# A hybrid decoder step: keys kept in token order, and the last weighting of a head pair put three slots after its weights

## Chip, cores and metric

One core of a Trainium2 chip runs the whole step. The metric is the device time of one execution in microseconds, the median of the runs shown; lower is better. One execution was also profiled, and its rows stand further down.

## What is computed

One layer for a prompt of 2048 tokens and a group of 8 samples with 4 new tokens each, model width 1024. The layer adds three mixers to its input through one output projection, and then a feed-forward network with a short convolution:

```python
x <- x + W_out[ concat(A, B, C) ](RMSNorm(x));   x <- x + ConvFFN(RMSNorm(x))
# A: 8 heads x 64, three (window, dilation) patterns, keys at distances 0, d, 2d, ..
PATTERNS = ((128, 1), (512, 4), (2048, 16))
oa = combine_dilations([dilated_band_prompt(qa, ka, va, slopes, w, d) for w, d in PATTERNS])
# combine_dilations:
mx = max over the patterns; num = sum(n * exp(m - mx)); den = sum(d * exp(m - mx)); out = num / den
# B: gated DeltaNet, 4 heads, chunks of 64;   C: cross-attention, 4 heads, 256 memory tokens
```

The keys of mixer A, after their RMS norm, are also an output (`win_k_prompt`), and so is every value row.

## The kernel before

**Precision.** A dense product is made of three matmuls (`mm3`, lines 294 to 296): a high part and a low part of each operand, the high part written by the Scalar engine (ACT), the low part by a subtraction on the Vector engine (DVE) or, for some weights, on GpSimd (POOL) (`weight`, lines 285 and 287).

**First stage** (`dense_in`, up to about 1040 us): the input projection of four blocks of 512 tokens, the DeltaNet, and the attention of the first 512 queries (`pair`, chunk 0). `head_norm` scales the heads' keys and queries; its `finish` makes the last product (line 499) and stores it. For keys the product is written into another tile (`vt`), its 512 tokens turned from token order into residue order (16 residues of 32 tokens), and stored so in `kT`. `vt` is a tag of three buffers; the values' evacuations (line 589), which come next in `ORDER`, need it too.

**Second stage** (`feed`): output projection and feed-forward network of one block after the other, and beside it the attention of the next block's 512 queries (chunks 1 to 3, three in all), issued in slots: `tick` lets one slot be issued after a share of the dense chunks. In `attn` a chunk's four head pairs and two cross pairs are a list of stages; stage k starts in slot k, and each of its functions stands one slot after the one before it. A head pair has six stages: load, far, middle (two halves), near (two halves). Its load splits the keys of two blocks for each of two heads (`ksplit`, lines 1130 and 1131, after `dup` has loaded `nat`, a tag of two buffers), four splits a pair. `far_scores` (line 1495) multiplies single residues of queries and keys, 256 matmuls a chunk as the trace counts them.

**The end of a pair.** `combine` (from line 1512) works out the weights of the two partial sums from small tiles, turns them on TensorE, copies them on ACT (`wt`, line 1535), sends them to DRAM (`wd`, line 1537) and brings them back spread over 128 partitions (`W`, line 1540). `finish_pair` then multiplies both partial sums by `W` on DVE (`os` line 1549, `nf` line 1550), adds them on POOL (line 1551) and stores the sum. `nf` has one buffer; the next pair's `mid_out` writes it from PSUM (`evac`, line 1088 on DVE). `add_halves` (line 1324, POOL) adds the two halves of `E` after their exponentials; TensorE transposes that sum (line 1319).

**Order.** The code's order gives priorities alone: a scheduler that runs when the kernel is built sets every engine's order, from its own estimates of the operations. Each engine and the queue of SyncE (SP), which issues all DMAs, then runs in that order, and what waits holds up what stands behind it.

Of the kernel before, what the change touches and what calls it, by code (L numbers as in the profile page):

```python
# [10 lines left out]
F32 = mybir.dt.float32  # L11
# [9 lines left out]
SEQ = 2048  # L21
# [44 lines left out]
def constants():  # L66
# [30 lines left out]
    with np.errstate(divide='ignore'):  # L97
# [8 lines left out]
        key = np.concatenate([128 * t + tok for t in range(4)])  # L106
        c['lbias'] = np.stack([bias(p[:, None] + 384 - key[None, :], sl) for sl in slopes])
        near = p[:, None] + 128 - key[None, 0:256]
# [97 lines left out]
def finish(r):  # L206
    y = r['yT'].reshape(D, TOT).T
    kT = r['kT'].reshape(512, TOT)
    kp = kT[:, :SEQ].reshape(512, SEQ // 512, 16, 32).transpose(0, 1, 3, 2).reshape(512, SEQ)
    kk = np.ascontiguousarray(np.concatenate([kp, kT[:, SEQ:]], 1).T)  # L210
# [19 lines left out]
class Body:  # L230
# [225 lines left out]
    def head_norm(self, srcs, xs, r4, w, gain, dsts, pre=(), turned=False):  # L456
# [31 lines left out]
        def finish():  # L488
            for x, raw in enumerate(raws):
                out = self.vt()[:, 0:w] if turned else raw  # L490
                for lo in range(0, w, 512):
# [3 lines left out]
                    o, i = out[:, lo:hi], raw[:, lo:hi]  # L495
                    if turned and lo == 0:
                        o = o.rearrange('p (r i) -> p i r', r=16)
                        i, ps = (t.rearrange('p (i r) -> p i r', r=16) for t in (i, ps))
                    nc.vector.scalar_tensor_tensor(out=o, in0=i, scalar=gain, in1=ps, op0=ALU.mult, op1=ALU.mult)
                for d, sl in dsts[x]:  # L500
                    nc.sync.dma_start(d, out[:, sl])
# [63 lines left out]
    def dense_in(self, b, xsr):  # L565
# [36 lines left out]
        def heads(c0, n, gain, dst, r4, pre=()):  # L602
            cols = lambda d: [(d[:, t0:t1], slice(0, npt))] + ([(d[:, SEQ:TOT], slice(npt, w))] if samp else [])
            return self.head_norm([A['w_ct'][c0 + x] for x in range(n)], xs, r4, w, gain, [cols(dst[x]) for x in range(n)], pre, dst is A['kT'])
# [475 lines left out]
    def neg(self, out, in_):  # L1080
        self.nc.vector.tensor_scalar(out=out, in0=in_, scalar1=-1.0, scalar2=None, op0=ALU.mult)
# [46 lines left out]
    def ksplit(self, src, kh, kl):  # L1128
        t = self.dup(src)
        self.nc.scalar.activation(kh, t, AF.Identity)  # L1130
        self.nc.vector.tensor_tensor(out=kl, in0=t, in1=kh.bitcast(F32), op=ALU.subtract)
# [70 lines left out]
    def cross_wide(self, c, hp):  # L1202
# [14 lines left out]
        def scores(n0):  # L1217
# [9 lines left out]
            self.neg(st[:, 0], st[:, 0])  # L1227
# [29 lines left out]
    def pair_load(self, c, hp):  # L1257
# [3 lines left out]
        for par in range(2):  # L1261
# [3 lines left out]
            for j in range(nb):  # L1265
                sl = slice(j * 512, j * 512 + 512)
                self.ksplit(self.A['kT'][hp, pr, (j0 + j) * 512:(j0 + j) * 512 + 512], *(t[:, sl] for t in K[par]))
        K = [[t.rearrange('p (b r i) -> p b r i', b=nb, r=16) for t in k] for k in K]
# [4 lines left out]
    def pair(self, c, hp):  # L1273
# [3 lines left out]
        v = self.values_of(range(4), cols)  # L1277
# [655 lines left out]
```

## Time and profile before

| | us |
|---|---|
| median of 3 runs | 2933.63 (2927.24 to 2937.6) |
| the profiled execution | 2932.09 |
| its span in the profile | 2930.3 |
| TensorE busy (matmul) | 2810.9, 96% |
| DVE, ACT, POOL busy | 2124.8, 1299.4, 902.2 |
| mean granted TensorE clock | 0.98 |

The span is the time from the first to the last instruction of the profiled execution; 1.8 us lie around it. The share of an engine is a mean over stages that differ, so the rows further down take it by stage. A granted clock of 1.00 is 2.4 GHz; parts of a stretch at 0.5 (1.2 GHz) pull its mean down.

### The profile page before, as it was taken

The numbers are of one execution on the slowest core, as the hardware profiler recorded it, in microseconds if no ns is written. First come the engines' busy times: TensorE is split into PE (matmuls) and PEld (weight loads), VectorE is DVE, ScalarE is ACT, GpSimd is POOL, SyncE is SP. The second block draws the span as 40 slices with busy tenths as digits, with TensorE's granted clock in tenths as the row PEclk, the third lists the DMA queues.
The fourth block names the chain that finished last, engine by engine and source line by source line (L and its number), as shares of the span: only waits on it lengthen the run. The fifth ranks groups of instructions, "written<-read, shape, count | busy, mean of one in ns | idle before, by whom it ended". The sixth has DMA issues, their size and how long they took to land. (4 is left out here: it accounts for less than half of the span.)

```text
span 2930.3 us, 55986 instructions
## 1 busy us (share of the span) xinstructions
PE 2810.9 (96%) x20702; PEld 2351.8 (80%) x20702; DVE 2124.8 (73%) x4696; ACT 1299.4 (44%) x2813; POOL 902.2 (31%) x1142
## 2 busy tenths in 40 slices
PE   8998989999989998999999989999899999999999
PEld 7778878777767777777677877777778778999999
DVE  7876747868756878778366888866877776666666
ACT  6545426546534435544233555435444433433332
POOL 3421302311312424333123343322333322333332
PEclk9999989999989999999999999999999999999999
DMA  5545423533434345544855545455444335232223
GB/s 175 161 133 95 141 82 125 165 111 115 130 109 131 97 117 147 152 139 132 269 180 169 151 142 150 137 170 171 135 151 140 103 93 168 94 90 91 87 87 102
DMA packets 275778, 390.88 MB, mean 133 GB/s; under 512 B 83952, under 2 KB 153744, under 8 KB 275504
## 3 DMA queue, kind: packets, MB, share of 16 engines
q1 hardware_dynamic: 275504, 387.29, 44.0%
q8 instruction: 164, 2.69, 0.4%
q14 instruction: 110, 0.90, 0.1%
HBM read 341.87 MB, written 45.32 MB: 132 GB/s over the span
## 5 line engine op out<-in xcount | busy, mean ns | idle before, releaser
L285 ACT ACTIVATE wh<-raw 128x512 fp32r<-128x512 f32 (+2 forms) x778 | 483.5, 626 | 716.4 <-PE facc L295 562.3
L294 PE MATMUL facc<-fh,wh 128*128 128x512 f32 (+1 forms) x2080 | 740.5, 357 | 11.2 <-DVE up L1868 5.4
L296 PE MATMUL facc<-fh,wl 128*128 128x512 f32 (+1 forms) x2080 | 737.6, 355 | 0.0
L295 PE MATMUL facc<-fl,wh 128*128 128x512 f32 (+1 forms) x2080 | 736.7, 355 | 0.7 <-DVE fl L356 0.7
L287 POOL TENSOR_TENSOR wl<-raw,wh 128x512 fp32r<-128x512 f32 (+1 forms) x259 | 356.1, 1375 | 839.9 <-ACT wh L285 741.6
L287 DVE TENSOR_TENSOR wl<-raw,wh 128x512 fp32r<-128x512 f32 (+2 forms) x519 | 369.5, 713 | 137.6 <-ACT wh L285 126.0
L294 PEld LDWEIGHTS facc<-fh,wh 128*128 128x128 f32 x2080 | 394.4, 190 | 67.9 <-issue 7.7
L296 PEld LDWEIGHTS facc<-fh,wl 128*128 128x128 f32 x2080 | 395.1, 190 | 55.5 <-issue 3.2
L295 PEld LDWEIGHTS facc<-fl,wh 128*128 128x128 f32 x2080 | 395.4, 190 | 53.5 <-issue 2.3
L1879 DVE SCALAR_TENSOR_TENSOR ca<-up,cwf,ca 128x512 f32<-128x512 f32 (+1 forms) x352 | 299.2, 855 | 30.1 <-ACT ca L1877 26.2
L294 PE MATMUL facc<-hH,wh 128*128 128x512 f32 (+1 forms) x880 | 312.2, 355 | 2.9 <-DVE y L1908 1.3
L295 PE MATMUL facc<-hL,wh 128*128 128x512 f32 (+1 forms) x880 | 311.7, 354 | 0.1
L296 PE MATMUL facc<-hH,wl 128*128 128x512 f32 (+1 forms) x880 | 311.1, 354 | 0.0
L294 PE MATMUL acc<-xh,wh 128*128 128x512 f32 (+1 forms) x720 | 260.1, 363 | 11.3 <-ACT wh L285 10.8
L296 PE MATMUL acc<-xh,wl 128*128 128x512 f32 (+1 forms) x720 | 259.2, 363 | 1.0 <-DVE wl L287 1.0
L295 PE MATMUL acc<-xl,wh 128*128 128x512 f32 (+1 forms) x720 | 259.8, 362 | 0.0
L1908 DVE TENSOR_TENSOR y<-y,facc 128x512 f32<-128x512 f32 (+1 forms) x240 | 139.8, 583 | 103.8 <-PE facc L296 102.9
L294 PEld LDWEIGHTS facc<-hH,wh 128*128 128x128 f32 x880 | 165.8, 189 | 28.6 <-issue 5.4
L296 PEld LDWEIGHTS facc<-hH,wl 128*128 128x128 f32 x880 | 166.0, 189 | 22.4 <-issue 0.9
L295 PEld LDWEIGHTS facc<-hL,wh 128*128 128x128 f32 x880 | 165.8, 188 | 22.4 <-issue 0.6
L1877 ACT ACTIVATE ca<-up,cwf 128x512 f32<-128x512 f32 (+1 forms) x176 | 127.5, 731 | 117.1 <-DVE up L1868 79.5
L1868 DVE TENSOR_TENSOR up<-facc,rows 128x512 f32<-128x512 f32 (+3 forms) x252 | 125.8, 514 | 64.8 <-PE facc L296 63.6
(491 smaller groups left out, 4864.5 us busy)
## 6 DMA issues: line engine op xcount, KB each, us to landing
raw<-in_w_up SPq DMA_DIRECT2D x176, 512.0 KB, 3.5
raw<-in_w_down SPq DMA_DIRECT2D x88, 512.0 KB, 3.7
raw<-in_w_ct SPq DMA_DIRECT2D x69, 512.0 KB, 3.7
raw<-in_w_out SPq DMA_DIRECT2D x32, 512.0 KB, 4.2
xr<-in_xT SPq DMA_DIRECT2D x56, 256.0 KB, 3.1
nat<-out_kT SPq DMA_DIRECT2D x112, 128.0 KB, 3.0
v<-out_win_v SPq DMA_DIRECT2D x172, 64.0 KB, 2.7
sV<-in_cv SPq DMA_DIRECT2D x40, 256.0 KB, 3.4
```

Source lines behind the costliest of these rows:

```text
L285: nc.scalar.activation(h, r, AF.Identity)
L287: (nc.gpsimd if self.wsel % self.wmod == 0 else nc.vector).tensor_tensor(out=l, in0=r, in1=h.bitcast(F32), op=ALU.subtract)
L294: mm(ps, lh, rh, start=first, stop=False)
L295: mm(ps, lh, rl, start=False, stop=False)
L296: mm(ps, ll, rh, start=False, stop=last)
L1868: nc.vector.tensor_tensor(out=dst, in0=src, in1=rr, op=ALU.mult)
L1877: nc.scalar.activation(ca, u[:, 0:n], AF.Identity, scale=self.cw_[:, ct, 0:1])
L1879: nc.vector.scalar_tensor_tensor(out=ca, in0=u[:, d:d + n], scalar=self.cw_[:, ct, d:d + 1], in1=ca, op0=ALU.mult, op1=ALU.add)
L1908: nc.vector.tensor_tensor(out=ys[m][:, sl], in0=ys[m][:, sl], in1=ps, op=ALU.add)
```

## The change

Keys are stored in token order. Where a later chunk's load splits them, both the ACT copy and the DVE subtraction now read token order and write residue order. Chunk 0 uses them in token order, and so its values come in one DMA and its bias table is in token order too. `far_scores` takes one residue of the keys by a step of 16 elements. `combine` moves one slot forward (it no longer stands after `near_out(2)` but in `near_turn(2)`), and `finish_pair` one slot back. The two DVE products of `finish_pair` may not be issued on DVE before the last negated maximum (`neg`) that was issued ahead of it in the code.

```diff
     def head_norm(...):
         def finish():
             for x, raw in enumerate(raws):
-                out = self.vt()[:, 0:w] if turned else raw
                 for lo in range(0, w, 512):
...
-                    o, i = out[:, lo:hi], raw[:, lo:hi]
-                    if turned and lo == 0:
-                        o = o.rearrange('p (r i) -> p i r', r=16)
-                        i, ps = (t.rearrange('p (i r) -> p i r', r=16) for t in (i, ps))
-                    nc.vector.scalar_tensor_tensor(out=o, in0=i, scalar=gain, in1=ps, op0=ALU.mult, op1=ALU.mult)
+                    nc.vector.scalar_tensor_tensor(out=raw[:, lo:hi], in0=raw[:, lo:hi], scalar=gain, in1=ps, op0=ALU.mult, op1=ALU.mult)
                 for d, sl in dsts[x]:
-                    nc.sync.dma_start(d, out[:, sl])
+                    nc.sync.dma_start(d, raw[:, sl])
...
-    def ksplit(self, src, kh, kl):
+    def ksplit(self, src, kh, kl, turned=False):
         t = self.dup(src)
+        if turned:
+            t = t.rearrange('p (i r) -> p r i', r=16)
+            kh, kl = (k.rearrange('p (r i) -> p r i', r=16) for k in (kh, kl))
         self.nc.scalar.activation(kh, t, AF.Identity)
         self.nc.vector.tensor_tensor(out=kl, in0=t, in1=kh.bitcast(F32), op=ALU.subtract)
...
     def pair(self, c, hp):
-        v = self.values_of(range(4), cols)
+        v = self.vp.tile([128, 4, 128], F32, tag='v', name='v')
+        nc.sync.dma_start(v, A['win_v'][0:512].rearrange('(n p) c -> p n c', p=128)[:, :, cols])
...
-                    nc.tensor.matmul(S, Q[par][:, n * 128:n * 128 + 128], K[par][x][:, 0].rearrange('p r (t i) -> p t r i', i=8)[:, 0:nk],
-                                     start=x == 0, stop=x == 1)
+                    nc.tensor.matmul(S, Q[par][:, n * 128:n * 128 + 128], K[par][x][:, 0:nk * 128], start=x == 0, stop=x == 1)
...
     def wide_pair(self, c, hp):
         def near_turn(n0):
             g['P', n0] = self.halves(g['E', n0], self.tmask)
+            if n0:
+                self.combine(hp, c, g['os'], g['ls'], (g['nf'], g['fst'].rearrange('p n s h -> p s h n')))
...
-        def end():
-            near_out(2)
-            self.combine(hp, c, g['os'], g['ls'], (g['nf'], g['fst'].rearrange('p n s h -> p s h n')))
...
-                [one(near_scores, 2), one(near_turn, 2), end, None, self.finish_pair]]
+                [one(near_scores, 2), one(near_turn, 2), one(near_out, 2), None, None, self.finish_pair]]
...
     def far_scores(self, c, hp, fb, kT, qf):
-                    nc.tensor.matmul(S[rr * 32:rr * 32 + 32, par, g, 0:nk], qf[pr, r::16], kT[pr, :, r], start=True, stop=True)
+                    nc.tensor.matmul(S[rr * 32:rr * 32 + 32, par, g, 0:nk], qf[pr, r::16], kT[pr, r::16], start=True, stop=True)
...
     def finish_pair(self):
-        tt(out=os_, in0=os_, in1=W[:, 0], op=ALU.mult)
-        tt(out=nv, in0=nv, in1=W[:, 1].rearrange('p (i r) -> p i r', r=16), op=ALU.mult)
+        with self.tc.issue_after(self.last.ins):
+            tt(out=os_, in0=os_, in1=W[:, 0], op=ALU.mult)
+            tt(out=nv, in0=nv, in1=W[:, 1].rearrange('p (i r) -> p i r', r=16), op=ALU.mult)
         nc.gpsimd.tensor_tensor(out=o3, in0=o3, in1=nv, op=ALU.add)
```

The scheduler's order differs from the first microseconds on, on every engine. Two places matter below.

DVE, the end of the first head pair of chunk 1, before (`fnm` is the negated maximum of the next pair's middle scores, `os` and `nf` are multiplied by `W`):

```order
L1376 TENSOR_TENSOR fs<-fnm,fm 128x2x2
L287 TENSOR_TENSOR wl<-raw,wh 128x512
L1879 SCALAR_TENSOR_TENSOR ca_14279<-up,cwf,ca_14279 128x512
L1081 TENSOR_SCALAR fnm<-fs 128x4
L1886 TENSOR_TENSOR hf<-ca_14236,ca_14279 128x512
L1868 TENSOR_TENSOR up<-facc,rows 128x512
L1549 TENSOR_TENSOR os<-os,W 128x512
L1550 TENSOR_TENSOR nf<-nf,W 128x32x16
L1893 TENSOR_TENSOR hL<-hf,hH 128x512
```

and now:

```order
L1373 TENSOR_TENSOR fs<-fnm,fm 128x2x2
L1905 TENSOR_TENSOR y_11711<-y_11711,facc 128x512
L1074 TENSOR_SCALAR fnm<-fs 128x4
L1546 TENSOR_TENSOR os<-os,W 128x512
L1329 TENSOR_TENSOR pt<-pT,c_mmask 128x512 x2
L1547 TENSOR_TENSOR nf<-nf,W 128x32x16
L285 TENSOR_TENSOR wl<-raw,wh 128x512
L1905 TENSOR_TENSOR y_11753<-y_11753,facc 128x512
L1381 TENSOR_TENSOR fs<-fden 128x2x2
L285 TENSOR_TENSOR wl<-raw,wh 128x512
L1081 COPY nf<-pT 128x2x4x32
```

The products stood behind the first half's maximum and stand now behind the second half's; the next pair's write of `nf`, which must wait for the POOL sum, stands four rows behind them here (28 before).

POOL at the same place, before (`os<-os,nf` is the pair's sum, `E<-E` the sum of two halves):

```order
L1324 TENSOR_TENSOR E<-E 128x2x128
L1875 COPY hist<-up 128x2
L1551 TENSOR_TENSOR os<-os,nf 128x512
L1324 TENSOR_TENSOR E<-E 128x2x128
L287 TENSOR_TENSOR wl<-raw,wh 128x512
```

and now:

```order
L285 TENSOR_TENSOR wl<-raw,wh 128x512
L1321 TENSOR_TENSOR E<-E 128x2x128
L1548 TENSOR_TENSOR os<-os,nf 128x512
L1321 TENSOR_TENSOR E<-E 128x2x128 x3
L285 TENSOR_TENSOR wl<-raw,wh 128x512
```

The pair's sum still has sums of halves behind it.

## Rows read from the trace of the kernel before

**Rows 1.** The page: busy time, share of the span, instructions of TensorE.

```profile
PE 2810.9 (96%) x20702; PEld 2351.8 (80%) x20702; DVE 2124.8 (73%) x4696; ACT 1299.4 (44%) x2813; POOL 902.2 (31%) x1142
```

**Rows 2.** Windows by stage: us; PE, PEld, DVE, ACT, POOL busy; PEclk; DMA share; GB/s.

```profile
0.00:1040.00 1040.00, 974.70 (x7909) 802.04 (x7910) 751.17 (x1908) 502.60 (x1061) 267.03 (x353) 0.97 0.43 126
1040.00:1360.00 320.00, 303.73 (x2209) 243.63 (x2208) 253.01 (x590) 153.12 (x404) 110.58 (x124) 0.96 0.48 140
...
1620.00:1910.00 290.00, 276.82 (x1939) 224.43 (x1938) 242.03 (x538) 145.46 (x392) 110.93 (x126) 0.99 0.48 145
...
2010.00:2370.00 360.00, 344.88 (x2188) 279.31 (x2187) 290.19 (x621) 176.23 (x431) 128.66 (x153) 0.99 0.43 128
```

**Rows 3.** Waits of PE: who waited for whom, us in total, times, longest.

```profile
PE pT L1319 <- POOL E L1324: 17.0, 15, 3.4
...
PE acc L294 <- ACT vt L589: 2.1, 2, 1.8
```

**Rows 4.** Waits of DVE: the row of W.

```profile
DVE os L1549 <- DMA W<-wd: 37.7, 12, 5.3
```

**Rows 5.** Timeline of the first pair's end: start, us, instruction, idle before it and releaser.

```profile
1150.38 0.39 PE L295 MATMUL facc<-fl,wh 128*128 128x512 f32 x1
...
1151.93 0.69 DVE L1549 TENSOR_TENSOR os<-os,W 128x512 f32<-128x512 f32 x1 [2.69 <-DMA W<-wd]
...
1153.75 1.90 POOL L1551 TENSOR_TENSOR os<-os,nf 128x512 f32<-128x512 f32 x1 [2.69 <-DVE nf L1550]
...
1155.61 1.24 POOL L1324 TENSOR_TENSOR E<-E 128x256 f32<-128x256 f32 x1
...
1156.91 0.69 PE L1319 MATMUL pT<-c_ident,E 128*128 128x128 f32 x2 [3.39 <-POOL E L1324]
...
1158.25 0.63 PE L295 MATMUL facc<-fl,wh 128*128 128x512 f32 x1
```

**Rows 6.** Windows around the twelve ends of a pair, columns as in rows 2.

```profile
1149.00:1162.00 13.00, 9.61 (x41) 7.54 (x40) 10.25 (x17) 7.27 (x21) 7.62 (x8) 0.87 0.45 121
1207.00:1230.00 23.00, 21.51 (x136) 17.49 (x135) 15.90 (x39) 12.79 (x42) 8.71 (x10) 0.85 0.34 96
1264.00:1290.00 26.00, 21.98 (x132) 17.53 (x131) 21.37 (x45) 12.11 (x43) 9.83 (x13) 0.80 0.31 87
...
2336.00:2352.00 16.00, 14.04 (x62) 11.22 (x62) 12.05 (x17) 6.69 (x17) 6.14 (x6) 0.89 0.36 87
sum 181.00, PE 160.83 PEld 129.34 DVE 135.30 ACT 81.52 POOL 80.64; mean PE 13.40 PEld 10.78 DVE 11.28 ACT 6.79 POOL 6.72
```

**Rows 7.** Groups by line and form: count, busy us, mean ns, idle before.

```profile
L1131 DVE TENSOR_TENSOR kl<-nat,kh 128x512 fp32r<-128x512 f32 x56 | 39.9, 713 | 26.9 <-ACT kh L1130 26.8
...
L1142 DVE TENSOR_TENSOR qh<-nat,qh 64x512 fp32r<-64x512 f32 x48 | 35.4, 739 | 28.2 <-ACT qh L1141 27.0
...
L1141 ACT ACTIVATE qh<-nat 128x512 fp32r<-128x512 f32 x48 | 29.9, 626 | 44.6 <-DMA nat<-qd 41.1 <-PE pS L1223 1.6 <-DMA nat<-qcd 1.4
...
L1142 DVE TENSOR_TENSOR qm<-nat,qm 64x512 fp32r<-64x512 f32 x24 | 28.3, 1177 | 3.7 <-ACT qm L1141 3.2
...
L1141 ACT ACTIVATE qm<-nat 128x512 fp32r<-128x512 f32 x24 | 26.3, 1095 | 0.4 <-PE pT L1395 0.4
...
L499 DVE SCALAR_TENSOR_TENSOR vt<-hraw,c_gm,st 128x512 f32<-128x512 f32 x16 | 17.4, 1108 | 0.8 <-PE st L494 0.8
...
L499 DVE SCALAR_TENSOR_TENSOR hraw<-hraw,c_gm,st 128x512 f32<-128x512 f32 x24 | 17.0, 739 | 0.0
```

**Rows 8.** Groups of PEld: weight loads of 32 columns.

```profile
L1495 PEld LDWEIGHTS pS<-kT,qf 64*32 64x32 f32 x768 | 10.4, 138 | 4.3 <-issue 2.5 <-DVE up L1868 0.4 <-PE facc L295 0.4
...
L1052 PEld LDWEIGHTS g<-sS,sqm 64*32 64x32 f32 x64 | 3.7, 107 | 0.0
```

**Rows 9.** Groups of PE: far scores of the longest form.

```profile
L1495 PE MATMUL pS<-kT,qf 64*32 64x96 f32 x256 | 4.9, 256 | 0.0
```

**Rows 10.** Line 1372: what TensorE waited for before the middle scores.

```profile
  ACT kh L1130: 3.3, 4
```

More of the change, by code (lines that the diff above doesn't have):

```diff
@@ L105, in constants @@
         tok = 16 * (p % 8) + p // 8
-        key = np.concatenate([128 * t + tok for t in range(4)])
-        c['lbias'] = np.stack([bias(p[:, None] + 384 - key[None, :], sl) for sl in slopes])
-        near = p[:, None] + 128 - key[None, 0:256]
+        key = np.concatenate([tok, 128 + tok])
+        c['lbias'] = np.stack([bias(p[:, None] + 384 - np.arange(512)[None, :], sl) for sl in slopes])
+        near = p[:, None] + 128 - key[None, :]
         mp = 4 * (p % 32) + p // 32
@@ L207, in finish @@
     y = r['yT'].reshape(D, TOT).T
-    kT = r['kT'].reshape(512, TOT)
-    kp = kT[:, :SEQ].reshape(512, SEQ // 512, 16, 32).transpose(0, 1, 3, 2).reshape(512, SEQ)
-    kk = np.ascontiguousarray(np.concatenate([kp, kT[:, SEQ:]], 1).T)
+    kk = np.ascontiguousarray(r['kT'].reshape(512, TOT).T)
     mk = np.ascontiguousarray(r['mkT'].reshape(256, NMEM).T)
@@ L454, in norm_quads, with head_norm @@
         return r4
-    def head_norm(self, srcs, xs, r4, w, gain, dsts, pre=(), turned=False):
+    def head_norm(self, srcs, xs, r4, w, gain, dsts, pre=()):
         nc = self.nc
@@ L603, in heads @@
             cols = lambda d: [(d[:, t0:t1], slice(0, npt))] + ([(d[:, SEQ:TOT], slice(npt, w))] if samp else [])
-            return self.head_norm([A['w_ct'][c0 + x] for x in range(n)], xs, r4, w, gain, [cols(dst[x]) for x in range(n)], pre, dst is A['kT'])
+            return self.head_norm([A['w_ct'][c0 + x] for x in range(n)], xs, r4, w, gain, [cols(dst[x]) for x in range(n)], pre)
         qkv = self.dram.tile([512, 768], F32, name=f'qkv{b}')
@@ L1080, in neg @@
     def neg(self, out, in_):
-        self.nc.vector.tensor_scalar(out=out, in0=in_, scalar1=-1.0, scalar2=None, op0=ALU.mult)
+        return self.nc.vector.tensor_scalar(out=out, in0=in_, scalar1=-1.0, scalar2=None, op0=ALU.mult)
     def evac(self, out, in_):
@@ L1226, in scores @@
             nc.vector.tensor_reduce(out=st[:, 0], in_=S, axis=AX.X, op=ALU.max)
-            self.neg(st[:, 0], st[:, 0])
+            self.last = self.neg(st[:, 0], st[:, 0])
             for x in range(2):
@@ L1266, in pair_load @@
                 sl = slice(j * 512, j * 512 + 512)
-                self.ksplit(self.A['kT'][hp, pr, (j0 + j) * 512:(j0 + j) * 512 + 512], *(t[:, sl] for t in K[par]))
-        K = [[t.rearrange('p (b r i) -> p b r i', b=nb, r=16) for t in k] for k in K]
+                self.ksplit(self.A['kT'][hp, pr, (j0 + j) * 512:(j0 + j) * 512 + 512], *(t[:, sl] for t in K[par]), turned=c > 0)
+        if c:
+            K = [[t.rearrange('p (b r i) -> p b r i', b=nb, r=16) for t in k] for k in K]
         ls = self.p2.tile([128, 2, 2, 4], F32, tag='ls', name='ls')
@@ L1376, in mid_scores @@
             nc.vector.tensor_tensor(out=fmx[:, gs], in0=mn[:, gs], in1=g['fm'][:, gs], op=ALU.max)
-            self.neg(mn[:, gs], fmx[:, gs])
+            self.last = self.neg(mn[:, gs], fmx[:, gs])
             for x in range(2):
@@ L1482, in far_load @@
         nc.sync.dma_start(qf, self.qd[hp, :, c * 512:c * 512 + 512])
-        return fb, kT.rearrange('p (b r i) -> p b r i', b=c, r=16), qf
+        return fb, kT, qf
     def far_scores(self, c, hp, fb, kT, qf):
```

## The prediction, on record before the changed kernel ran

> **What bounds the kernel now.** I read the page first: TensorE is busy 96% of the span [rows 1], so a microsecond counts only where TensorE stands still or runs at its lower clock, and the question for each edit is whether it changes one of the two. Then I cut the span by stage [rows 2]. TensorE is idle 1040 - 974.7 = 65.3 us in the first stage and 16.3, 13.2 and 15.1 us in the three stretches in which the attention of chunks 1, 2 and 3 runs beside the dense work. The mean granted clock is 0.97, 0.96, 0.99, 0.99: of 1.00 (2.4 GHz) that is some 31, 13, 3 and 4 us of full-speed time lost to stretches at 1.2 GHz. So 65 us of the 110 us idle and 31 us of the 51 us of clock lie in the first stage, and only 45 us and some 20 us where head pairs of chunks 1 to 3 run. That is all the change's second half can reach.
>
> Then the waits. The largest one of TensorE there is for POOL's sum of two halves, 17.0 us in 15 waits [rows 3], and DVE stands still 37.7 us in 12 waits for the DMA of W, once per pair, at most 5.3 us [rows 4]. The timeline of the first pair's end [rows 5] joins the two: DVE waits 2.69 us for W and starts the product of `os` at 1151.93; POOL, whose next row is the pair's sum, has waited the same 2.69 us and sums until 1155.65; only behind that comes the sum of halves, and TensorE, which needs it, has stood 3.39 us. Right after, the same dense matmul takes 0.63 us that took 0.39 us before: the granted clock had fallen to its lower level behind the idle time.
>
> **The weights earlier, the products later.** The stretches around all twelve pair ends [rows 6] price this. Over 181.0 us TensorE is busy 160.83, so idle 20.2 us; the clock loses 13 x 0.13 + 23 x 0.15 + 26 x 0.20 + 16 x 0.11 = 12.1 us in the four that are not at 1.00. So at most 32 us hang on the ends of the pairs, and at least nothing: in some stretches a wait of DVE cost TensorE under 1 us. Does the change take the waits away? In the new order each distance on DVE from the first small product of the weights to the product with W grows by 5 to 50 rows, by 5 where the wait was 2.69 us, by 10 or more where it was largest in chunk 1. In chunk 1 a DVE row stands for 320 / 590 = 0.54 us [rows 2], so five rows are 2.7 us: the waits should all but vanish. What is late next? The order on POOL still has the pair's sum ahead of sums of halves, and that sum took 1.90 us [rows 5]. But the products now stand right behind the maximum that releases ACT's exponentials, so the POOL sum runs while the exponentials do, and these have to end first anyway. In the one timeline that I followed, 2.69 of 3.39 us would go; elsewhere idle time near a pair end has other releasers too. I take half of 32: **-16 us**, with ends 0 and -32.
>
> The forced order adds a wait, DVE's products on the maximum ahead of them; that is on DVE itself, so it costs nothing unless W is late. New is also that the next pair's copy into `nf`, one buffer, now stands four to eleven rows behind the product at nine places and waits for POOL's sum. Behind it on DVE are the masks (`pt`) that TensorE waits for. The rows between (two products into `y` or splits, a split and a small sum in the tightest case) take some 0.7 us each for the large ones [the split's kind in rows 7], over 2 us in all, against 1.9 us of POOL: I take 0, and up to 0.7 us at nine places = 6 us if POOL is in the middle of something. The queue of SP has no more to do: its store of `os` waits for POOL as before, and chunk 0 saves 12 small DMAs that nobody waited for.
>
> **Keys split by a turned read.** Of the 56 long splits 48 belong to chunks 1 to 3 (3 chunks, 4 pairs, 4 each) and now read with a step of 16 elements. The trace has the same operation in both forms, for the queries [rows 7]: ACT 1095 ns turned and 626 plain, DVE 1177 and 739 (the keys' plain one 713). So ACT gets 48 x 0.469 = 22.5 us and DVE 48 x 0.438 = 21.0 us more. ACT is busy 153 of 320 us in chunk 1 and DVE 253 [rows 2], so both have room, and DVE gives back 37.7 us of standing. What hides it is the distance of two slots between a load and the first middle scores; where that cover ends shows in the trace: TensorE waited for `kh` before the middle scores 4 times of 12, 3.3 us [rows 10]. Bounds: 0 (a longer split makes nothing earlier), and 43.5 us if every nanosecond on both engines came before TensorE. The nearest row is rows 10: four pairs already at the limit, each later by two of its four splits, 4 x 0.94 = 3.8. I take **+4 us**.
>
> **Far scores by a step of 16.** No row shows a moving operand read so. From below 0 (a contiguous read is not slower than a stepped one; the columns hide behind 32-column weight loads). The stationary side is stepped already: 138 ns against 107 ns for a contiguous load of the same size [rows 8], 29% more. The three forms are busy at most 3 x 4.9 = 14.7 us [rows 9]; 29% of it is 4.3 us, all of it again 14.7 us. I take **+2 us**, half of the nearest row's price.
>
> The Trainium skill ("Advanced Engine Details and Errata", Memory Cachelines) speaks against this side of the change: SBUF is read in lines of 16 bytes, and a read that has only one element in a line pays, which a step of 16 fp32 elements does. The trace agrees for ACT and DVE (1095 against 626 ns). The page gives no size; by it the sum would move towards the upper ends, and the second rival would gain.
>
> **Stores of keys, chunk 0.** The last product of the key heads loses its turned write: 1108 to 739 ns, 16 times, 5.9 us of DVE [rows 7]. No `vt` buffer is held by the store any more, so the values' evacuation loses its wait, which TensorE saw as 2.1 us [rows 3]; the raw tiles are held until the store instead, but a whole head's or value product lies before their next use. I take **-2 us**, ends -2.1 and 0. Beside that, the scheduler gives the whole first stage another order: 65.3 us idle and 31 us of clock are dealt anew there, and I can put no sign on it: 10 us either way in the range.
>
> **Sum.** -16 + 4 + 2 - 2 = -12 us on the profiled execution's 2932.09 us is 2920.1. That execution lies 1.5 us under the median of the three runs (2933.63), so as a median 2921.6: **2922 us**.
>
> **The rivals.**
> 1. *The wait goes, the time stays.* POOL's sum still stands ahead of the halves' sums, and `nf` now waits for it; DVE's freed time is off the path. For it: only some of the waits cost TensorE anything; the largest ones in chunk 3 none. Then 0 to -4 from the ends of the pairs, and +4 + 2 - 2: 2932 to 2938, **2934**. Against it: rows 5.
> 2. *Slower: the turned splits are late.* `nat` has two buffers, and every turned split holds one longer by 0.469 + 0.438 = 0.91 us, four in a row per pair, so that the first middle scores wait for `kh` and `kl` in all pairs and TensorE's clock falls with them. At three quarters of 43.5 us on the path: +33 - 16 + 2 - 2 = +17: **2950**. It decides from (16 + 8.8) / 43.5 = 57% on the path on. For it: 4 of 12 pairs are at the limit, and the skill's page above. Against it: two slots of cover.
> 3. *More than half.* All waits at the pair ends and the clock's dips behind them go, and the new first stage is no worse: -32 + 2 + 0 - 2: **2902**.
> 4. *The order is not what the text says* (products still ahead of W): the built order excludes it, all twelve distances grew; no chance of its own.
>
> **How the numbers follow.** 0.3% of 2933.6, 8.8 us, is about what a measurement of this kernel can tell from no change: faster is under 2924.8, slower over 2942.4. The forecast, 2906 to 2924.8, gets 0.42; more than that (rival 3) 0.11; rival 1, with the cases in which the first stage's new order eats the gain, 0.29; rival 2, with a first stage that turns out 10 us worse, 0.18. So faster 0.53, same 0.29, slower 0.18. The range: 2900 leaves out 0.06 below, and 2945 leaves out 0.13 above, part of rival 2.
>
> **What would show it.** DVE's wait for W under 5 us in all; the waits of TensorE for POOL's sum of halves under 10 us; chunk 1's stretch with a clock above 0.96 and idle time under 12 us; turned splits at about 1.1 us on ACT and 1.15 on DVE; waits for `kh` before the middle scores under 8 us; far scores at no more than 1.3 times their busy time. I am wrong if `kh` waits pass 15 us, if POOL's sum keeps TensorE waiting as long as now, or if the first stage's idle time moves by more than 10 us, which nothing here foresees.

## The result, and the profile after

The changed kernel takes **2884.7 us** (median of four runs, 2883.8 to 2887.59) against 2933.82 of the kernel before: a ratio of 0.9837 [0.9818, 0.9856]. Run again on another occasion it came to 2889.72 against 2933.51, 0.9853 [0.9839, 0.9868]. So 44 to 49 us went, where 12 were forecast, and 2884.7 lies below the range of 2900 to 2945. The profiled execution has a span of 2882.7 us.

TensorE's share on the page, against [rows 1]:

```profile
PE 2788.4 (97%) x20702; PEld 2339.4 (81%) x20702; DVE 2132.5 (74%) x4696; ACT 1317.7 (46%) x2811; POOL 924.0 (32%) x1142
```

The waits of TensorE, against [rows 3] and [rows 10] (who waited for whom, us in total, times, longest):

```profile
PE pT L1316 <- POOL E L1321: 13.3, 9, 4.1
...
PE pS L1369 <- ACT kh L1126: 5.1, 5, 2.3
```

DVE's wait for W [rows 4], 37.7 us, is gone; the wait for POOL's sum of halves has only fallen from 17.0 to 13.3 us; the wait for `kh` before the middle scores has risen from 3.3 to 5.1. None of this is near 49 us. The first place where the time shows is the span cut at each block's first output-projection split on ACT. Before (columns as in rows 2):

```profile
0.00:862.00 862.00, 798.08 (x6836) 664.00 (x6836) 611.73 (x1612) 425.82 (x916) 210.78 (x290) 0.97 0.44 128
862.00:1386.00 524.00, 506.35 (x3396) 402.78 (x3397) 413.99 (x914) 240.79 (x567) 178.04 (x200) 0.97 0.44 131
```

and after:

```profile
0.00:814.00 814.00, 767.08 (x6516) 644.56 (x6516) 593.72 (x1606) 422.47 (x911) 211.81 (x290) 0.99 0.47 135
814.00:1346.00 532.00, 512.53 (x3705) 408.39 (x3706) 423.62 (x919) 247.36 (x569) 186.42 (x200) 0.97 0.43 129
```

The first mark is not a clean one: 6516 matmuls stand ahead of it instead of 6836, so some work has only moved behind it. At the second mark both have issued about the same (10,232 and 10,221): 1386 has become 1346, **40 us of the 48 us of span**. The block up to the third output projection gives nothing (543.1 us before, 543.6 after), the one up to the fourth 7 us (514.8, 507.7), the last stage 1.

Inside the first stage one stretch stands out. From 366 to 439 us, before:

```profile
366.00:439.00 73.00, 61.32 (x699) 52.87 (x698) 31.49 (x95) 21.10 (x50) 4.67 (x6) 0.82 0.29 82
```

and after:

```profile
366.00:439.00 73.00, 71.39 (x917) 63.84 (x916) 43.82 (x134) 34.00 (x77) 9.25 (x9) 1.00 0.40 119
```

In the same 73 us TensorE now does 917 matmuls instead of 699. Before, it was idle for 11.7 us and lost 73 x 0.18 = 13.1 us to the lower clock, 24.8 us together; now 1.6 us and nothing.

What happens in it before can be followed on ACT (start, us, instruction, idle before it and releaser):

```profile
388.68 0.47 ACT L589 ACTIVATE vt<-acc,nr 128x256 f32<-128x256 f32 x1 [2.39 <-DMA out_win_v<-vt]
...
401.93 0.63 ACT L1141 ACTIVATE qh<-nat 128x512 fp32r<-128x512 f32 x1 [9.89 <-DMA nat<-qd]
406.70 0.63 ACT L1130 ACTIVATE kh<-nat 128x512 fp32r<-128x512 f32 x1 [4.14 <-DMA nat<-out_kT]
407.24 0.57 ACT L929 COPY uw<-g 128x512 f32<-128x512 f32 x1
```

and one row of TensorE in the same place:

```profile
407.86 1.13 PE L936 MATMUL g<-ka,uw 64*64 64x128 f32 x16 [4.63 <-ACT uw L929]
```

ACT runs in order. TensorE makes the product that the DeltaNet's copy `uw` reads from 399.7 us on, but on ACT two splits of chunk 0 stand ahead of this copy, and they wait for loads that SyncE issued at 398.4 and 403.3 us. TensorE, with nothing else that is ready, stands 4.63 us; the same matmul of 256 columns (L295) took 0.28 us ahead of it and 0.41 us behind it, at the lower clock. After, the copy stands ahead of the splits:

```profile
402.17 0.59 ACT L922 COPY uw<-g 128x512 f32<-128x512 f32 x1 [0.78 <-PE g L920]
...
412.12 0.63 ACT L1137 ACTIVATE qh<-nat 128x512 fp32r<-128x512 f32 x1 [2.39 <-DMA nat<-qd]
```

That is the scheduler's order, and not a wait for a buffer. The only wait of ACT for a buffer of `vt` in this stretch is the 2.39 us in the first row, and it is for a store of values. A store of keys holds ACT up elsewhere, and longer than TensorE ever showed:

```profile
ACT vt L589 <- DMA out_kT<-vt: 12.4, 6, 7.0
```

These six waits lie at 604 to 607 and 819 to 821 us, and the row is absent after. From 560 to 640 and 800 to 840 us TensorE lost 19 us before, idle time and clock together, and 12 after; in the stretch it is 24.8 and 1.6, and from 680 to 720 and 840 to 880 us 13 and nothing. [rows 3] has only TensorE's own part of the waits, 2.1 us.

### The profile page after: what moved, and what is told of

It is laid out like the page before. It is cut to its first block, busy times and chain, and to the rows that moved or that the text cites. A ratio compares the mean times of both kernels' runs of the same rounds, so it can differ in the third digit from the quotient of the medians.

```text
span 2882.7 us, 56002 instructions
## 1 busy us (share of the span) xinstructions
PE 2788.4 (97%) x20702; PEld 2339.4 (81%) x20702; DVE 2132.5 (74%) x4696; ACT 1317.7 (46%) x2811; POOL 924.0 (32%) x1142
## 5 line engine op out<-in xcount | busy, mean ns | idle before, releaser
L285 DVE TENSOR_TENSOR wl<-raw,wh 128x512 fp32r<-128x512 f32 (+2 forms) x519 | 376.9, 728 | 108.7 <-ACT wh L283 100.3
L293 PEld LDWEIGHTS facc<-fl,wh 128*128 128x128 f32 x2080 | 394.9, 190 | 55.8 <-issue 3.5
L1860 POOL COPY up<-hist 128x2 f32<-128x2 f32 x176 | 74.9, 426 | 291.8 <-DVE ca L1876 228.5
```

What stands on the lines that cost most here:

```text
L285: (nc.gpsimd if self.wsel % self.wmod == 0 else nc.vector).tensor_tensor(out=l, in0=r, in1=h.bitcast(F32), op=ALU.subtract)
L293: mm(ps, lh, rl, start=False, stop=False)
L1860: nc.gpsimd.tensor_copy(u[:, 0:2], self.hist[:, ct])
```

## The experiments

Differences in us are against the median of the kernel before in the same series of runs (2928.3 to 2933.5). What is compared across two series is good to some 10 us, as one of the runs shows. `vt` is the tag that key products and values share.

### Each half of the change alone

The keys' part alone, with the pair ends as before:

```diff
-            if n0:
-                self.combine(hp, c, g['os'], g['ls'], (g['nf'], g['fst']...))
+        def end():
+            near_out(2)
+            self.combine(hp, c, g['os'], g['ls'], (g['nf'], g['fst']...))
...
-        with self.tc.issue_after(self.last.ins):
-            tt(out=os_, ...); tt(out=nv, ...)
+        tt(out=os_, ...); tt(out=nv, ...)
```

> Keys' part of the change alone; the end of a head pair is as before (weights after near_out, products unforced, one slot earlier). Its first stage stands in the changed kernel's order on TensorE and DVE. Theory 1 (the gain is the keys' part, made in the first stage): 2885 to 2898, out_proj of the first block starts near 814 us as in the changed kernel, DVE's wait for W is back at some 35 us, and chunks 1 to 3 are 0 to 10 us longer. Theory 2 (the gain is the end of a pair, as the prediction had it): 2915 to 2940, because turned splits cost and nothing at the pair ends is gained. By the prediction's own terms: 2932 + 4 + 2 - 2 = 2936.

Measured: 2912.85 us, 0.9946 [0.9928, 0.9964], **-17.7 us**. Its second output projection starts at 1355.9 us (1385.5 before), and the two blocks behind it take 4.7 and 4.6 us more than before: the turned splits and the stepped far scores cost there somewhat more than was forecast (6 us for all three chunks), and the gain lies ahead of them. The whole came out between the two theories.

The pair ends alone, in the kernel before:

```diff
+            if n0:
+                self.combine(hp, c, ...)
...
-                [one(near_scores, 2), one(near_turn, 2), end, None, self.finish_pair]]
+                [one(near_scores, 2), one(near_turn, 2), one(near_out, 2), None, None, self.finish_pair]]
...
+        with self.tc.issue_after(self.last.ins):
```

> End of a pair alone: weights one slot earlier, products one slot later and forced behind the last maximum; keys as before (residue order, turned store, plain splits). Its first stage stands in the order of the kernel before. Theory 1: 2920 to 2934 (the first stage unchanged, out_proj of the first block near 862 us; at most 10 us gained in chunks 1 to 3, DVE's wait for W gone). Theory 2: 2885 to 2905. By the prediction's own term: 2933.8 - 16 = 2918.

Measured: 2910.5 us, 0.9933 [0.9914, 0.9951], **-20.0 us**, between the two theories; run a second time as a reference for a later experiment:

> The end of the pair alone in the kernel before, a second time, as the reference for the kernel beside it. First measured at 2910.5 us, ratio 0.9933 [0.9914, 0.9951]; expected again 2906 to 2916 us.

Measured: 2912.44 us, 0.9931 [0.9913, 0.995], -20.1. The forecast's term for this half was -16. The other half was to cost 4 us and gains 18; that is where the forecast failed.

### What the first stage gained: a new order, or a buffer?

A null edit shows what a small change of the order is worth: two independent products of the DeltaNet written in the other sequence.

```diff
-        nc.vector.tensor_tensor(out=v4(sc3[:, 0]), in0=q, ...)
         nc.vector.tensor_tensor(out=v4(sc3[:, 1]), in0=q, ...)
+        nc.vector.tensor_tensor(out=v4(sc3[:, 0]), in0=q, ...)
```

> The kernel before with two independent DVE products in gdn_tile (lines 775 and 776) written in the other order: nothing added or taken away, but the scheduler's order differs from the DeltaNet of the second block on. Theory C (a new order of the first stage alone moves the time by tens of us): it moves by more than 10 us either way. Theories A and B: within 8 us of before, 2926 to 2942.

Measured: 2931.11 us, 1.0007 [0.9994, 1.0019], +0.6. By the traces it moved 22 rows of DVE, the first at 549 us, and none of ACT and POOL, so it tells little of a first stage that is drawn anew. Next, in the kernel before, the turned key product goes into another tag:

```diff
-                out = self.vt()[:, 0:w] if turned else raw
+                out = self.dc.tile([128, 571], F32, tag='ca', name='kout')[:, 0:w] if turned else raw
```

> The kernel before, but the turned key product goes into a tile of the tag ca (three buffers, of the raw heads and the convolution) and not of vt; residue order, four value DMAs and the end of a pair stay. Theory A (the gain is that the values' evacuations no longer wait for vt): 2890 to 2912, ACT's wait for out_kT<-vt gone, first stage 25 to 45 us shorter. Theory B (what else the keys' part does: the plain product, one value DMA for a chunk-0 pair, plain reads): 2925 to 2940, first stage within 10 us of before. Theory C (any other order of the first stage would do): anywhere from 2890 to 2950, with no tie to vt waits.

Measured: 2915.33 us, 0.9954 [0.9935, 0.9973], **-15.2 us**, with nothing else of the change in it, though 3 us short of the range of theory A. ACT's wait for stores of keys is gone. And the reverse, the changed kernel with its key product through `vt` (in token order):

```diff
+                out = self.vt()[:, 0:w] if turned else raw
...
-                    nc.vector.scalar_tensor_tensor(out=raw[:, lo:hi], in0=raw[:, lo:hi], ...)
+                    nc.vector.scalar_tensor_tensor(out=out[:, lo:hi], in0=raw[:, lo:hi], ...)
```

> The changed kernel, but the key product goes through vt again (in token order, plain write): only the hold on vt is put back. Theory A (the keys' part gains because the values' evacuations no longer wait for vt): 2898 to 2912, ACT's wait for out_kT<-vt back near 12 us. Theory B (the plain product, one value DMA, plain reads): 2880 to 2890. Theory C (chance of the order): anywhere.

Measured: 2914.84 us, 0.9956 [0.9939, 0.9973], only -13.5, 3 us above theory A's range. Its second output projection starts at 1372.4 us, 27 us later than in the changed kernel; of the whole gain 21 us are given back against the variant with four value DMAs in the same series (below), and 30 to 35 against the changed kernel in two others. These three can still be read in two ways, as the run's waits for the buffer or as the order that the scheduler makes without it. So one more takes the *values* out of `vt` and leaves the keys in it:

```diff
-                    t = self.vt()[0:m, 0:256]
+                    t = self.dc.tile([128, 571], F32, tag='ca', name='vth')[0:m, 0:256]
```

> The kernel before with one word changed: the second half of the values is evacuated into a buffer of the tag ca instead of vt; the key product stays in vt. Theory buffer (the values' evacuations wait on ACT until the keys have left vt, and all that stands behind them on ACT waits too): ACT's wait for out_kT<-vt, 12.4 us in 6 waits, falls under 4 us, the second output projection starts before 1370 us (1385.5 before), and the whole is 10 to 20 us below the kernel before. Theory order (it was the order that the scheduler happened to make): within 5 us of the kernel before, even with the wait gone. The tag ca has users of its own; if they are held up in turn, the time rises and the run tells nothing.

Measured: 2912.62 us, 0.9938 [0.992, 0.9956], **-20.8 us**; the second output projection starts at 1349.3 us, almost as early as in the changed kernel (what it then loses again, 14 us, goes in the block from there to the third one, with TensorE idle for 19.5 us of it instead of 15.5 and the clock at 0.97 instead of 0.99). ACT's wait for stores of keys is gone, but now it waits 11.3 us for stores of values in their new tag, 5.5 us of that at 367 and 385 us. The stretch from 366 to 439 us is fast all the same, and the copy stands ahead of the splits in it:

```profile
384.87 0.47 ACT L589 ACTIVATE vth<-acc,nr 32x256 f32<-32x256 f32 x1 [3.67 <-DMA out_win_v<-vth]
...
398.60 0.59 ACT L929 COPY uw<-g 128x512 f32<-128x512 f32 x1 [2.82 <-PE g L927]
...
404.17 0.63 ACT L1141 ACTIVATE qh<-nat 128x512 fp32r<-128x512 f32 x1 [3.50 <-DMA nat<-qd]
```

That stretch, TensorE's idle time in the first 1040 us, the place of the copy on ACT (behind or ahead of the next two splits) and the start of the second output projection, in one profiled execution of each program:

| keys and values | program | matmuls, 366 to 439 us | clock | idle, 0 to 1040 us | `uw` | second output projection |
|---|---|---|---|---|---|---|
| both in `vt` | before | 699 | 0.82 | 65.3 | behind | 1385.5 |
| | null edit | 696 | 0.84 | 73.3 | behind | 1387.9 |
| | pair ends alone (second run) | 644 | 0.81 | 68.8 | behind | 1381.4 |
| | pair ends alone, weights late (below) | 661 | 0.81 | 70.1 | behind | 1384.7 |
| | change, keys in `vt` | 738 | 0.86 | 61.2 | behind | 1372.4 |
| apart | keys in `ca` | 902 | 1.00 | 51.2 | ahead | 1364.9 |
| | values in `ca` | 889 | 1.00 | 49.4 | ahead | 1349.3 |
| | keys' part alone | 914 | 1.00 | 51.2 | ahead | 1355.9 |
| | change | 917 | 1.00 | 49.8 | ahead | 1345.8 |
| | change, weights late (below) | 909 | 1.00 | 52.2 | ahead | 1343.6 |

The halves do not overlap. The five programs of the upper half have one order: up to 439 us the traces show the same rows on TensorE, DVE, ACT and POOL, even with most of the change in (the last of the five). Those of the lower half have three different orders (keys in `ca`, values in `ca`, and the three with the keys' part), and all three put the copy first. So the shared tag is shown as the cause, from either side of it, and what it acts through is the order that the scheduler makes: ACT waits 5.5 us for a buffer in a fast stretch, and 2.4 and 2.1 us (before, and the change with keys in `vt`) in slow ones. The waits themselves are worth little: the places from 560 to 640 and 800 to 840 us, where the stores of keys hold ACT, cost TensorE 19 to 21 us in the upper half and 12 to 16 in the lower. Why the scheduler puts the copy behind the splits when the tag is shared isn't shown, and what changed from 680 to 720 and 840 to 880 us wasn't followed.

### Do the issues on SyncE count?

Chunk 0's values come in one DMA a pair instead of four. Undone in the changed kernel; the orders of the four compute engines stay the same:

```diff
-        nc.sync.dma_start(v, A['win_v'][0:512].rearrange('(n p) c -> p n c', p=128)[:, :, cols])
+        for n in range(4):
+            nc.sync.dma_start(v[:, n], A['win_v'][n * 128:n * 128 + 128, cols])
```

> The changed kernel, but a chunk-0 pair's values come in four DMAs again (in token order). TensorE, DVE, ACT and POOL keep the changed kernel's order row for row, only SP issues 12 more DMAs. Theory A: within 4 us of the changed kernel, 2881 to 2889. Theory B': SP's issue time (four DMAs took 2.88 us) holds up the loads of nat behind it: 2890 to 2900.

Measured: 2893.49 us, 0.9885 [0.9865, 0.9904], 9 us above the changed kernel's median of another series. Its profile lost most of that around 200 us, at a clock dip that none of these DMAs stands near, so it was run again beside the changed kernel:

> The changed kernel itself once more, so that the three kernels beside it are compared on one chip. Its ratio to the kernel before was 0.9837 [0.9818, 0.9856]; if that is the change and not the chip, the ratio comes out within 0.9815 to 0.986 again.

> The changed kernel with the values of chunk 0 loaded by four DMAs a pair as before, a second time, now beside the changed kernel on the same chip. The orders of TensorE, DVE, ACT and POOL are those of the changed kernel. Theory SP (the twelve issues removed from SyncE's queue are worth time): 8 to 15 us above the changed kernel's own median here. Theory chance (the first look at it fell 9 us behind in the DeltaNet stretch around 200 us, with a clock dip of 13.7 us that no DMA of chunk 0's values stands near; where the clock falls differs between executions): within 4 us of the changed kernel's median.

Measured: the changed kernel 2889.72 us, this one 2888.41, both 0.9853. The twelve issues are worth nothing that shows, and 9 us between two series mean nothing here.

### The pair ends: place, order, weights

The changed kernel without the forced order; both slots as changed:

```diff
-        with self.tc.issue_after(self.last.ins):
-            tt(out=os_, ...); tt(out=nv, ...)
+        tt(out=os_, ...); tt(out=nv, ...)
```

> The changed kernel without the forced place of the two products; weights one slot earlier and products one slot later stay. If the distance between weights and products does it: within 4 us of the changed kernel, DVE's wait for W under 5 us. If the forced place does it: 2892 to 2902, with DVE standing for W again or POOL's sum in front of the sums of halves for longer.

Measured: 2907.87 us, 0.993 [0.9909, 0.9952], -20.5: hardly more than the keys' part alone (-17.7), and a smaller gain than either theory had. DVE waits for W again, 8.4 us more of it at `nf`:

```profile
DVE os L1545 <- DMA W<-wd: 19.0, 8, 5.3
```

The scheduler had pulled the products back up. From the start of the weights' copy on ACT to the product of `os` it is 7 to 12 us in the kernel before, 7 to 17 here, and 10 to 41 in the changed kernel (start times of the twelve pairs). The later slot alone moves a priority and nothing more.

The forced order alone, with both slots as before (`end` is `near_out(2)`, then `combine`):

```diff
-                [one(near_scores, 2), one(near_turn, 2), one(near_out, 2), None, None, self.finish_pair]]
+                [one(near_scores, 2), one(near_turn, 2), end, None, self.finish_pair]]
```

> The changed kernel with both slots as before (weights after the near half's output, products two slots later), and only the forced order of the products left of the change at the pair ends. Theory order (it is the issue_after that puts the products behind the last negated maximum, where W has landed): 2876 to 2892 us, and DVE waits under 8 us for W. Theory slot (a slot earlier the last negated maximum comes earlier as well, and W has not landed by then): 2898 to 2912 us, as without the forced order, and DVE waits 15 us or more for W.

Measured: 2901.92 us, 0.9898 [0.988, 0.9915], -31.5, between the two theories: 14 us better than the keys' part alone, which has neither order nor slot, and 12 to 18 worse than the changed kernel. The wait of DVE is a third of what it was:

```profile
DVE os L1547 <- DMA W<-wd: 13.5, 5, 4.1
```

The last maximum comes earlier in that slot, and at five pairs W has not landed by then. Order and slot are both needed for the whole gain. The earlier weights aren't, as the next shows; products as changed, weights where they were:

```diff
-            if n0:
-                self.combine(hp, c, ...)
+        def end():
+            near_out(2)
+            self.combine(hp, c, ...)
...
-                [one(near_scores, 2), one(near_turn, 2), one(near_out, 2), None, None, self.finish_pair]]
+                [one(near_scores, 2), one(near_turn, 2), end, None, None, self.finish_pair]]
```

> The changed kernel with the weights worked out where they were before (after the near half's output instead of in the slot that turns the near half's exponentials); the products stay a slot later and in forced order. The scheduler finds another order for it in the second stage. Theory place (what counts is that the two products stand behind the last negated maximum on DVE, by when W has long landed): within 5 us of the changed kernel, DVE waits under 4 us for W. Theory weights (W lands just in time, the earlier weights are needed): 8 to 20 us above the changed kernel, and DVE waits for W again in 3 or more of the 12 pairs.

Measured: 2879.22 us, 0.9819 [0.9805, 0.9834], **-54.3: faster than the changed kernel beside it** (0.9853 [0.9839, 0.9868]) by 10.5 us, which neither theory had. No wait of DVE for W remains in it. Against chance of the order, the same in the kernel before's keys, beside the second run of the pair ends alone:

> The kernel before with the products a slot later and in forced order, and the weights left where they were, after the near half's output. Theory cost (the weights' transposes, copies and small DVE work in the earlier slot stand in the way of the near half's turn and output): 6 to 14 us below the kernel with the whole new end. Theory draw (the faster order in the changed kernel was chance): within 4 us of it, or above.

Measured: 2894.43 us, 0.9872 [0.9853, 0.9892], -38.1 against -20.1: 18 us better with the weights late, more than either theory had. Twice, in unlike orders, moving the weights forward cost 10 to 18 us. In both, most of it goes between the second and the third output projection. TensorE's waits there, changed kernel (second run):

```profile
PE pT L1316 <- POOL E L1321: 6.2, 4, 3.4
```

and with the weights late:

```profile
PE pT L1316 <- POOL E L1321: 0.7, 2, 0.5
```

(in the other couple 6.6 us and no such row; the two windows are 547 against 536 us, and 543 against 530). In one of the waits in the changed kernel POOL sums a pair for 2.50 us from 1774.50 us on, then the next pair's halves, and TensorE stands 3.45 us until 1778.18. It is the picture of [rows 5] once more, now without W in it: POOL's sum of a pair stands ahead of the next pair's sum of halves, and TensorE waits for the second. With the weights late the two stand in the same sequence on POOL, but TensorE has other work just then. Why the earlier weights bring the two together isn't settled.

### The two strided reads

The changed kernel with its splits not turned (the keys of chunks 1 to 3 are left in token order and are then multiplied in the wrong places; the work is the same but for the step of the reads):

```diff
-                self.ksplit(self.A['kT'][...], *(t[:, sl] for t in K[par]), turned=c > 0)
+                self.ksplit(self.A['kT'][...], *(t[:, sl] for t in K[par]))
```

> The changed kernel with plain splits in chunks 1 to 3: the keys keep token order there but are used as if in residue order, so the turn is left out of the computation and nothing else; every engine's order is the same row for row. The prediction's term (+4 us for the turn): 2879 to 2882. From the stages of the run with the keys' part alone (about 5 us longer per chunk): 2868 to 2874. If DVE and ACT time were on the path in full: 2845.

Measured: 2876.15 us, 0.9824 [0.9803, 0.9846], -52.2: 3 to 8 us below the changed kernel's -44 and -49 of other series, and 17 below the variant with four value DMAs in its own. So the turn costs 3 to 17 us. And the far scores with consecutive keys:

```diff
-        return fb, kT, qf
+        return fb, kT.rearrange('p (b r i) -> p b r i', b=c, r=16), qf
...
-                    nc.tensor.matmul(S[...], qf[pr, r::16], kT[pr, r::16], ...)
+                    nc.tensor.matmul(S[...], qf[pr, r::16], kT[pr, :, r], ...)
```

> The changed kernel with the far scores reading each residue's keys as consecutive elements, as if kT still lay in residue order; it lies in token order, so the far scores multiply the wrong keys. All orders are those of the changed kernel. The forecast's term for the step was +2, with 0 to +14.7 as ends; the far multiplications' busy time rose from 13.3 to 16.5 us. Expected by it: 1 to 5 us below the changed kernel. If the step costs more than the busy time shows (weights held up behind it): 8 to 15 us below.

Measured: 2887.68 us, 0.9851 [0.9833, 0.9869], against 0.9853 and 0.9837 of the changed kernel: nothing that shows either way. Here too wrong keys are multiplied, and the work is the same.

### An attempt to save issues

Each `nat` tile is filled by two DMAs from one source. Made one:

```diff
-        for e in range(2):
-            self.nc.sync.dma_start(t[e * 64:e * 64 + 64], src)
+        self.nc.sync.dma_start(t, src.unsqueeze(0).to_broadcast([2] + list(src.shape)))
```

> The changed kernel with the two DMAs that fill the halves of nat from the same source made one (120 issues fewer on SyncE, 24 of them in the first stage). The scheduler finds another order on every engine. Theory SP (issues on SyncE cost time while the first stage runs): 8 to 20 us below the changed kernel. Theory cover (SyncE is ahead of who needs its loads, TensorE is busy 97% of the span and its idle 90 us have other causes): within 6 us of it, and ACT's wait for nat<-out_kT, 53.2 us in the changed kernel, changes without moving the span.

Measured: 3247.08 us, 1.1077 [1.1059, 1.1095], **+313.6 us** against the kernel before, and 357 us above the changed kernel beside it, from which it differs by this edit. Neither theory had that. ACT's waits:

```profile
ACT kh L1125 <- DMA nat<-out_kT: 235.8, 47, 9.5
ACT qh L1136 <- DMA nat<-qd: 128.2, 23, 8.8
```

against 53.2 us for the first in the changed kernel. The section on the hardware says what the trace shows of it.

## Why the prediction was wrong

**The step that failed: in "Stores of keys, chunk 0", the first stage's new order, put at nothing.** The term has two parts. The first, -2, is the values' wait for a buffer that a store of keys holds, "which TensorE saw as 2.1 us". This wait is gone, and its size was not far off: the places where it stood lost 19 us before and lose 3 to 7 us less with the tag taken apart. The second part says that the scheduler "gives the whole first stage another order", that 65 us of idle time and 31 us of clock "are dealt anew", with "no sign" and "10 us either way", and so it is 0 in the sum. That was the larger part by far. With the tag taken apart alone the second output projection starts 21 and 36 us earlier and the whole gains 15 and 21 us; put back into the changed kernel, the sharing costs 21 to 35. The deal had a sign, because it was the shared tag that shaped the order: one copy of the DeltaNet stood behind two splits that waited for loads, and a fourteenth of the stage (73 of 1040 us) held a quarter of its loss (24.8 of 96 us). The place of this copy stands in both built orders, which the forecast read at the pair ends alone. The text named what would prove it wrong: "if the first stage's idle time moves by more than 10 us". It moved from 65.3 to 49.8 us over the first 1040 us.

**The pair ends, -16.** Measured alone, -20. The mechanism was right in the main: DVE's wait for W went (forecast under 5 us: no row left), and with the pair ends alone TensorE's wait for the sums of halves fell from 17.0 to 8.5 and 7.6 us in two runs (forecast under 10). In chunk 1 about the same work, the 2213 matmuls behind the first 7909, took 320.2 us before (315.3 with the null edit) and 305.7 and 306.9 with the pair ends alone, idle 11.7 and 9.7 us at a clock of 0.99 and 0.98, as was asked ("under 12", "above 0.96"). In the changed kernel the signs are missed but for the clock: POOL's sum still stands ahead of sums of halves, the wait is 13.3 us, and the same matmuls take 316.3 us, idle 16.4, clock 0.97. The keys' part alone has 325.2 us there, so it takes back much of what the pair ends give. That the size fits is in part luck. Earlier weights were counted as one of two means; they cost 10 to 18 us, and with them left alone the pair ends give -38, more than the upper end of 32. That end came from windows around the pair ends, so some of the gain must lie outside them. The forced order was costed at nothing, "on DVE itself", and is what makes the later slot work at all.

**Turned splits, +4.** ACT's form rose by 22.9 us and DVE's by 17.2 (forecast 22.5 and 21.0):

```profile
L1126 ACT ACTIVATE kh<-nat 128x512 fp32r<-128x512 f32 x56 | 58.1, 1037 | 65.9 <-DMA nat<-out_kT 53.2 <-PE pS L1437 12.7
L1127 DVE TENSOR_TENSOR kl<-nat,kh 128x512 fp32r<-128x512 f32 x56 | 57.1, 1019 | 18.8 <-ACT kh L1126 18.7
```

(the means mix 48 turned and 8 plain ones.) Some 40 us of work became 3 to 17 us of time. The forecast's 4 lies in that, but its size isn't shown; the rival that had the splits late, 2950, is out. The wait for `kh` stayed at 5.1 us, under the 8 forecast.

**Far scores, +2.** Measured: nothing that shows (0.9851 against 0.9853 and 0.9837); busy time rose from 13.3 to 16.5 us, 1.24 times, where at most 1.3 was forecast. The longest form, against [rows 9]:

```profile
L1491 PE MATMUL pS<-kT,qf 64*32 64x96 f32 x256 | 7.3, 341 | 0.0
```

Nearly half as long again for one form, and 29% was the estimate from the nearest row; small either way.

**The key product and the SyncE queue.** The product in place takes 740 ns, as forecast, and "12 small DMAs that nobody waited for" is right (0.9853 both).

**The sum.** The keys' part is -17.7 instead of +4, the pair ends -20 instead of -16: -38. The changed kernel has -44 to -49, so 6 to 11 us more came from the two together. With the weights late the parts add up (-17.7 - 38.1 = -55.8, measured -54.3), so the surplus may belong to the early weights, whose price came out as 10 us in the one order and 18 in the other; it is no more than what two series can differ by, and it isn't traced further. The third rival had the direction, "more than half", but for another reason: it stood on the pair ends and on a first stage "no worse".

## What to carry to other kernels

A tag that a store's source and the next evacuations share does two things: it can hold an engine up in the run, and it shapes the order that the scheduler makes. The trace names the first alone, and here the second was the larger. Before a forecast puts "another order" at nothing, take the stretch in which TensorE is idle and its clock is down, ask which row ends it, and look where that row stands in both built orders. Moving either side of a shared tag to another tag is a one-word experiment. Where a scheduler sets the order, a later slot is only a wish: look at the distance in the built order, and force it where it matters, but leave alone the producer that is already early enough.

## What the hardware showed unexpectedly

**One DMA for two halves.** Filling 128 partitions by one DMA whose source is read twice (a step of zero over an outer size of 2) cost 357 us over two DMAs of 64 partitions each (3247.1 against 2889.7 us, with the scheduler's order changed as well). Counted from the completion events in the trace, less than 3 us apart: in the changed kernel (second run) 1,526 of 1,553 groups have 16 events; in this one 1,119 have 16, 157 have 14, and 364 have one or two. In all there are 21,784 events where 1,459 DMAs of 16 would leave 23,344: 13 fewer for each of the 120 DMAs of this form. So these came in over few of the engines, and other DMAs, the groups of 14, had their last two completions late. The Trainium skill ("DMA: Bandwidth & Descriptors", Why a DMA increments its semaphore by 16 and not by 1) has the rule: the number of engines is the largest one up to 16 that divides the sizes of the slowest dimensions of both sides, so an outer size of 2 means 2 engines. By that rule the two halves of 64 get 16 each; the trace agrees, in that these have 16 events and the DMAs with an outer size of 2 have 3; what the third one is, the trace doesn't tell.

**Steps of 16 elements in fp32.** ACT's 128x512 split takes 1.10 us instead of 0.63, DVE's 1.07 instead of 0.71 (worked out from the means above, 48 of 56 turned), and a far matmul of 96 columns is busy for 341 ns instead of 256. The Trainium skill ("Advanced Engine Details and Errata", Memory Cachelines) has the direction, as the prediction said, and these are sizes for it; on the path, as the runs show, they were 3 to 17 us for the splits and nothing that shows for the far scores.
